# Feed-forward products as 2x2 blocks with seven products on two token chunks, middle features through DRAM

## The chip, the core and the metric

The kernel runs on one core of a Trainium2 chip. The metric is the time of one execution on the device, in microseconds (us), taken as the median of three runs. Five engines work side by side, each through its own instruction queue in order: TensorE (PE, matrix products, with its weight loads PEld), VectorE (DVE), ScalarE (ACT), GpSimd (POOL) and SyncE (SP, which here issues most transfers). Work of different engines is ordered by semaphores. Operands lie in SBUF (128 partitions), products accumulate in PSUM (8 banks), and everything else lies in DRAM.

## What is computed

One inference step of a two-layer decoder trunk: 1024 prompt tokens and 32 sample tokens, together T = 1056 columns, with 1024 features. Each layer mixes tokens (a recurrence, windowed attention, two gated branches), normalizes, and then runs the feed-forward part, which is all that changes here:

```python
x = layer_norm(ALPHA * x + mix @ P['w_out'], P['ln1_g'], P['ln1_b'])
h = jnp.square(jax.nn.relu(x @ P['w_ff_up']))
x = layer_norm(ALPHA * x + h @ P['w_ff_down'], P['ln2_g'], P['ln2_b'])
```

`w_ff_up` is 1024 x 4096 and `w_ff_down` is 4096 x 1024. All is float32.

## The kernel before

**Layout.** Activations are feature-major: a tile holds 128 features by the tokens of one chunk. The chunks `CH` are 384, 384 and 288 tokens wide. x is 8 such tiles per chunk (`KD`), the 4096 middle features are 32 (index f), in 8 groups of G = 4.

**Precision.** A float32 factor is split into a high part in a reduced format (`fp32r`) and the rest: `split` for activations and `wsplit` for weights do a cast on ACT (L257, L223) and a subtraction on DVE (L258, L224). A product is three matmuls: high x high, high x low, low x high. So one tile of 128 x 128 weights against one chunk costs three matmuls with 384 or 288 columns. `gemm_parts` (L233) issues them into one PSUM bank, and takes the banks of `gbanks` in turn: in the feed-forward part `mm` and `c`, two banks each.

**Feed-forward, `ff` (L1311).** For each group of 4 middle rows, `up` makes h for each row and chunk (24 matmuls; ACT takes the relu out of PSUM at L1320, DVE squares at L1321, then `split`), and h stays in SBUF. Then `down` adds that group's part to each of the 8 output rows (12 matmuls; DVE adds the bank to the accumulator in SBUF at L1335). One raw weight tile of 128 x 1024 is loaded by SP (L214) per up row and per pair of output rows, two raw buffers deep, and split into one of four weight tiles (three in `wp`, one in the small pool).

**Order.** Tile's scheduler orders the instructions of every engine at build time by readiness and by their order in the program. Inside `manual_schedule` PE's order is that of the program: there the rest of the output projection (`tail`), the three parts of the first normalization (booked into the stream of matmuls by `book` at the times `LN_TIMES`) and the first three up rows are woven. At the end the last group's `down` is woven with the second normalization in the same way. In between no POOL instruction is used.

**Slots.** `Slots` hands out SBUF tiles by chunk: `outer` 16 and `inner` 20 for each of the three chunks. `layer_norm` takes the sums on DVE and POOL and, for the first normalization, writes x as high and low parts (L337 to L342) and gives the float32 tile back (`acc[k].put()`).

Of the kernel before, what the change touches and what calls it, by code (L numbers as in the profile page):

```python
# [10 lines left out]
F32 = mybir.dt.float32  # L11
# [6 lines left out]
L = 2  # L18
# [92 lines left out]
class Kern:  # L111
    def __init__(self, tc, i, o, ctx):
# [15 lines left out]
        self.wpools = deque([self.wp])  # L128
        self.gbanks = deque([(self.mm, "mm")])
# [27 lines left out]
        self.d_g = [dt(f"d_g{l}", (16, 128, T)) for l in range(L)]  # L157

# [52 lines left out]

    def wraw(self, src):
        raw = self.rp.tile([128, 1024], F32, tag="raw", name=self.nm("raw"))
        self.nc.sync.dma_start(out=raw, in_=src)  # L214
        return raw

    def wsplit(self, raw):
        nc = self.nc
        pool = self.wpools[0]
        self.wpools.rotate(-1)  # L220
        w = pool.tile([128, 2, 8, 128], F32R, tag="w", name=self.nm("w"))
# [14 lines left out]
    def gemm_parts(self, w, k0, rhs, n):  # L236

        p = self.ps(*self.gbanks[0])
        self.gbanks.rotate(-1)
        nk = len(rhs)  # L240
        for k in range(nk):
            hi, lo = rhs[k]
            wh, wl = w[:, 0, k0 + k, :], w[:, 1, k0 + k, :]
            for j, (a, b) in enumerate(((wh, hi), (wh, lo), (wl, hi))):
                self.mmul(p[:, :n], lhsT=a, rhs=b[:, :n], start=(k == 0 and j == 0),
                          stop=(k == nk - 1 and j == 2))
                yield
        return p

# [35 lines left out]
    def layer_norm(self, tmp, small, acc, s, c, gcol, bcol, out=None, last=False):  # L285
# [47 lines left out]
        for k in range(KD):  # L333
# [3 lines left out]
            if out is None:  # L337
                hi, lo = self.outer.get(c, F32R), (self.outer if self.outer.free[c] else tmp).get(c, F32R)
# [3 lines left out]
                acc[k].put()  # L342
# [890 lines left out]
    def mix(self, l, inner, small):  # L1233
# [67 lines left out]
        def tail(c):  # L1301
# [4 lines left out]
            self.book(self.layer_norm(inner, small, [xf[k][c] for k in range(KD)], sums[c], c, P_L1G, P_L1B), LN_TIMES)  # L1306

        return tail


    def ff(self, l, inner, small, tail):  # L1311
        nc, tc, i = self.nc, self.tc, self.i
        ng = 32 // G
        sums = [None] * 3

        def up(w, h, f, c):
            n = CH[c][1]
            p = yield from self.gemm_parts(w, 0, self.xr(c), n)
            z, hi, lo = inner.get(c), inner.get(c, F32R), inner.get(c, F32R)
            nc.scalar.activation(out=z.f, in_=p[:, :n], func=AF.Relu)  # L1320
            nc.vector.tensor_tensor(z.f, z.f, z.f, op=ALU.mult)  # L1321
            self.split(z.f, hi.t, lo.t)
            z.put()
            h[f, c] = (hi, lo)

        def down(w, h, m, c, gi):
# [3 lines left out]
            if gi == 0:  # L1330
                hi, lo = self.x[m][c]
                nc.vector.scalar_tensor_tensor(a, hi.f, ALPHA, p[:, :n], op0=ALU.mult, op1=ALU.add)
                nc.vector.scalar_tensor_tensor(a, lo.f, ALPHA, a, op0=ALU.mult, op1=ALU.add)
            else:
                nc.vector.tensor_tensor(a, a, p[:, :n], op=ALU.add)  # L1335

        for gi in range(ng - 1):
            h = {}
            if gi == 0:
                with tc.manual_schedule(engines={mybir.EngineType.PE}):  # L1340
                    for c in range(3):
                        self.weave(tail(c))
                    ws = [self.wload(i["w_up"][l, f]) for f in range(3)]
                    for c in range(3):
                        for f in range(3):
                            self.weave(up(ws[f], h, f, c))
                    self.due()
                acc = [[inner.get(c) for c in range(3)] for _ in range(KD)]
            for f in range(3 if gi == 0 else 0, G):
                w = self.wload(i["w_up"][l, gi * G + f])  # L1350
                for c in range(3):
                    drain(up(w, h, f, c))
            for mp in range(4):
                w = self.wload(i["w_down"][l, gi, mp])
                for m in (2 * mp, 2 * mp + 1):
                    for c in range(3):
                        drain(down(w, h, m, c, gi))
            for f, c in h:
                for t in h[f, c]:
                    t.put()  # L1360
        h = {}
        self.wpools = deque([self.wp] * 3 + [small])
        for f in range(G):
            w = self.wload(i["w_up"][l, gi * G + G + f])
            for c in range(3):
                drain(up(w, h, f, c))
        ws = [self.wload(i["w_down"][l, ng - 1, mp]) for mp in range(4)]
        for r in self.x:
            for a, b in r:
                a.put()  # L1370
                b.put()
        self.x = [[None] * 3 for _ in range(KD)]
# [5 lines left out]
        with tc.manual_schedule(engines={mybir.EngineType.PE}):  # L1378
            for c in range(3):
                for m in range(KD):  # L1380
                    self.weave(down(ws[m // 2], h, m, c, ng - 1))
                    self.add_up(inner, sums, acc, m, c)
# [11 lines left out]
    def run(self):  # L1394
        nc, tc, i = self.nc, self.tc, self.i
        self.x = [[None] * 3 for _ in range(KD)]
        for l in range(L):
# [6 lines left out]
            with ExitStack() as ctx:  # L1404
# [4 lines left out]
                self.wpools = deque([self.wp] * 3 + [sp])  # L1409
                self.gbanks = deque([(self.mm, "mm"), (self.pc, "c")])  # L1410
                self.ff(l, inner, sp, self.mix(l, inner, sp))
            self.wpools = deque([self.wp])
            self.gbanks = deque([(self.mm, "mm")])
# [149 lines left out]
```

## Time and profile before

| | us |
|---|---|
| median of three runs | 3591.2 (3590.25 to 3594.06) |
| the profiled execution, its own time | 3581.97 |
| its span, first to last instruction | 3579.8 |
| PE busy | 3476.0 (97%) |
| DVE, ACT, POOL busy | 1980.9, 1100.0, 655.7 |

The profile is one execution. "Busy" of PE counts matmuls that overlap; how fast PE really goes is read from the chain of work, where 24 matmuls in a row have one length. The granted clock (PEclk) is a share of full speed. The feed-forward parts are the stretches from about 1020 to 1790 us and from about 2790 us to the end.

### The profile page before, as it was taken

How to read it: one execution, taken by the hardware profiler on the slowest of the kernel's cores; microseconds unless marked ns; L12 is line 12 of the kernel's file. 1: busy time of each engine (PE TensorE's matmuls, PEld its weight loads, DVE VectorE, ACT ScalarE, POOL GpSimd, SP SyncE). 2: the span in 40 equal slices, each digit the busy share in tenths (PEclk: the TensorE clock that was granted, in tenths of full speed). 3: DMA queues.
4: the chain of work that ended last, by engine and by line, in shares of the span. 5: the costliest groups of instructions: out<-in, count | busy, mean ns of one | idle time of the engine just before them, and what ended most of it. 6: DMA issues, size and time to landing. Idle time of an engine off the chain costs nothing.

```text
span 3579.8 us, 63696 instructions
## 1 busy us (share of the span) xinstructions
PE 3476.0 (97%) x25286; PEld 3226.5 (90%) x25286; DVE 1980.9 (55%) x5216; ACT 1100.0 (31%) x2553; POOL 655.7 (18%) x1014
## 2 busy tenths in 40 slices
PE   8999999998989999999999999999999899999997
PEld 8688888888989999999987888888799899999997
DVE  4746777756465333333657478777573643333335
ACT  4654332222152122212347443322221422221222
POOL 2223423210140000000342334232102300000002
PEclk9999999999999999999999999999899999999998
DMA  5124233325111111111131333222351111111111
GB/s 169 61 91 116 77 83 81 85 72 183 59 30 48 48 48 44 46 48 48 34 86 49 102 103 92 78 79 83 109 154 36 42 48 48 47 43 48 48 42 49
DMA packets 213225, 255.45 MB, mean 71 GB/s; under 512 B 103488, under 2 KB 175712, under 8 KB 212896
## 3 DMA queue, kind: packets, MB, share of 16 engines
q1 hardware_dynamic: 184032, 211.31, 20.3%
q10 hardware_dynamic: 27360, 35.57, 2.7%
q8 instruction: 199, 3.26, 0.4%
q0 software_dynamic: 1536, 4.52, 0.3%
q14 instruction: 98, 0.80, 0.1%
HBM read 188.99 MB, written 58.95 MB: 69 GB/s over the span
## 4 chain that ended last, share of the span: by engine, by line
PE 84%; DVE 5%; issue 1%; POOL 1%; ACT 1%; DMA 1%; SPq 0%; ACTq 0%; DVEq 0%; POOLq 0%
PE mm L202 44%; PE c L202 30%; PE b L202 8%; PE b L206 1%; DMA i<-d_ya 0%; PE c L206 0%; PE b L759 0%; DVE pd L985 0%; DVE Xt L987 0%; DVE x L1260 0%; POOL x L341 0%; DMA i<-d_yr 0%; DVE ln L270 0%; DVE ln L271 0%; DVE A L1022 0%
## 5 line engine op out<-in xcount | busy, mean ns | idle before, releaser
L202 PE MATMUL mm<-x,w 128*128 128x384 f32 (+1 forms) x7680 | 1439.4, 333 | 15.6 <-ACT x L257 6.8
L202 PEld LDWEIGHTS mm<-x,w 128*128 128x128 f32 x7680 | 1238.9, 190 | 68.9 <-issue 12.5
L202 PE MATMUL mm<-i,w 128*128 128x384 f32 (+1 forms) x3264 | 584.9, 323 | 17.4 <-ACT i L257 17.4
L202 PE MATMUL c<-i,w 128*128 128x384 f32 (+1 forms) x3264 | 582.4, 323 | 0.8 <-DVE i L1275 0.6
L202 PEld LDWEIGHTS mm<-i,w 128*128 128x128 f32 x3264 | 533.8, 189 | 21.1 <-ACT i L257 17.6
L202 PEld LDWEIGHTS c<-i,w 128*128 128x128 f32 x3264 | 534.2, 188 | 3.5 <-DVE i L1275 1.2
L223 ACT CAST w<-raw 128x1024 fp32r<-128x1024 f32 x232 | 243.0, 1048 | 738.3 <-PE c L202 526.2
L202 PE MATMUL c<-x,w 128*128 128x384 f32 (+1 forms) x2496 | 439.1, 324 | 0.0
L202 PEld LDWEIGHTS c<-x,w 128*128 128x128 f32 x2496 | 410.3, 190 | 0.4 <-DVE x L258 0.4
L224 DVE TENSOR_TENSOR w<-raw,w 128x1024 fp32r<-128x1024 f32 x232 | 287.1, 1237 | 98.0 <-ACT w L223 96.3
L1321 DVE TENSOR_TENSOR i<-i 128x384 f32<-128x384 f32 (+1 forms) x192 | 101.1, 527 | 348.0 <-ACT i L1320 348.0
L283 POOL TENSOR_TENSOR i<-i,i 128x384 f32<-128x384 f32 (+1 forms) x36 | 36.4, 1012 | 1377.1 <-DVE i L1335 1372.9
L1335 DVE TENSOR_TENSOR i<-i,c 128x384 f32<-128x384 f32 (+1 forms) x168 | 87.3, 520 | 197.2 <-PE c L202 197.2
L1335 DVE TENSOR_TENSOR i<-i,mm 128x384 f32<-128x384 f32 (+1 forms) x168 | 87.0, 518 | 133.8 <-PE mm L202 133.7
L258 DVE TENSOR_TENSOR i<-i,i 128x384 fp32r<-128x384 f32 (+1 forms) x216 | 116.9, 545 | 77.6 <-ACT i L257 77.5
L257 ACT CAST i<-i 128x384 fp32r<-128x384 f32 (+1 forms) x216 | 104.7, 486 | 91.2 <-DVE i L1321 80.9
L787 POOL TENSOR_TENSOR z<-z,gs 128x384 f32<-128x384 f32 (+1 forms) x84 | 80.1, 953 | 287.2 <-issue 185.2
L1320 ACT ACTIVATE i<-mm 128x384 f32<-128x384 f32 (+1 forms) x96 | 44.7, 465 | 208.5 <-PE mm L202 208.5
L1103 DVE SCALAR_TENSOR_TENSOR S<-c,eL,sd 64x64 f32<-64x64 f32 x256 | 72.4, 283 | 63.3 <-PE c L202 58.9
L1320 ACT ACTIVATE i<-c 128x384 f32<-128x384 f32 (+1 forms) x96 | 44.7, 465 | 200.6 <-PE c L202 200.6
L1093 DVE COPY sav<-c 64x128 f32<-64x128 f32 x128 | 36.8, 288 | 125.3 <-PE c L202 124.3
L1079 POOL TENSOR_SCALAR sd<-S,eL 128x128 f32<-128x128 f32 x128 | 96.8, 757 | 49.2 <-DVE S L1103 46.2
(278 smaller groups left out, 3982.8 us busy)
## 6 DMA issues: line engine op xcount, KB each, us to landing
raw<-in_w_in_dram SPq DMA_DIRECT2D x72, 512.0 KB
raw<-in_w_up_dram SPq DMA_DIRECT2D x64, 512.0 KB
raw<-in_w_down_dram SPq DMA_DIRECT2D x64, 512.0 KB
d_g<-gs ACTq DMA_DIRECT2D x64, 192.0 KB
i<-d_g SPq DMA_DIRECT2D x64, 192.0 KB
d_z<-z ACTq DMA_DIRECT2D x52, 192.0 KB
raw<-in_w_out_dram SPq DMA_DIRECT2D x16, 512.0 KB
qrot<-qraw SPq DMA_DIRECT2D x40, 132.0 KB
```

Of the source, the lines that this page charges most:

```text
L202: return self.nc.tensor.matmul(out, lhsT=lhsT, rhs=rhs, start=start, stop=stop)
L223: nc.scalar.copy(wf[:, 0, :], raw)
L224: self.weng.tensor_tensor(wf[:, 1, :], raw, wf[:, 0, :].bitcast(F32), op=ALU.subtract)
L257: self.nc.scalar.copy(hi, src)
L258: self.nc.vector.tensor_tensor(lo, src, hi.bitcast(F32), op=ALU.subtract)
L787: nc.gpsimd.tensor_tensor(out[:, :n], out[:, :n], prev[:, :n], op=ALU.add)
L1079: nc.gpsimd.tensor_scalar(sd, S0, ecol, None, op0=ALU.mult)
L1093: nc.vector.tensor_copy(sav[B, :], sa[B, 0:128])
L1103: nc.vector.scalar_tensor_tensor(S1[r, r], pS[r, 0:64], ecol[r, :], sd[r, r], op0=ALU.mult, op1=ALU.add)
L1320: nc.scalar.activation(out=z.f, in_=p[:, :n], func=AF.Relu)
L1321: nc.vector.tensor_tensor(z.f, z.f, z.f, op=ALU.mult)
L1335: nc.vector.tensor_tensor(a, a, p[:, :n], op=ALU.add)
```

## The change

The feed-forward products over the first two chunks (384 tokens each) are made as 2 x 2 blocks with seven block products in place of eight. For **up**, a pair of middle rows (f, f+1) is one side of the block, the two halves of x's 8 tiles the other, and the two chunks the third. For **down**, a pair of output rows, two and two of a group's 4 middle tiles, and the two chunks. Chunk 2 (288 tokens) keeps its plain products, and so do the first 4 up rows and the last down group.

What comes with it:

- `tokens_up` makes four differences of x per k (8 on POOL, 8 on DVE) and splits them, once in a layer; x must stay in float32 until then (`keep`, which also stores it in DRAM as `d_x`, from where `residual` loads it).
- `weights_up` makes for each pair of rows four sums of 128 x 512 on POOL, and splits 3.5 weight tiles in place of 2. `weights_down` makes four sums of 128 x 256 on POOL for each pair of output rows and splits 2 tiles in place of 1.
- The banks are combined on their way out: `pair_up` has an ACT copy, 7 DVE additions and 2 ACT relus per pair, then relu (ACT) and square (POOL) for the four tiles in `store`; every middle tile goes to DRAM (`d_h`).
- `tokens_down` loads a group's 12 middle tiles back, makes 8 differences of 128 x 384 on POOL, and splits 14 tiles of 384 and 4 of 288 columns. It comes after the group before in the program.
- `pair_down` keeps seven accumulators per pair of output rows (`E`), with one DVE addition per block product; chunk 2 goes out by an ACT copy and a POOL addition (in group 0 by one DVE instruction). `finish` combines the seven after group 6.
- Four more buffers: raw tiles and weight tiles also in the small pool (4 and 5 in all), and seven-product banks in the order `mm`, `b`, `c`, `b`, so all 8. The DMA scratch is cut to 2048 bytes.

```diff
 def wraw(self, src):
-        raw = self.rp.tile([128, 1024], F32, tag="raw", name=self.nm("raw"))
+        raw = self.rtile()
...
+    def products(self, ops, n):
+        p = self.ps(*self.gbanks[0])
+        self.gbanks.rotate(-1)
+        e = len(ops) - 1
+        for q, (w, k, (hi, lo)) in enumerate(ops):
+            for j, (a, b) in enumerate(((0, hi), (0, lo), (1, hi))):
+                self.mmul(p[:, :n], lhsT=w[:, a, k, :], rhs=b.t[:, :n], start=(q == 0 and j == 0), stop=(q == e and j == 2))
+        return p[:, :n]
...
-                acc[k].put()
+                if keep is None:
+                    acc[k].put()
+                else:
+                    nc.sync.dma_start(out=keep[k, :, c0:c0 + n], in_=a[k])
...
+        def store(z, f, c):
+            nc.scalar.activation(out=z.f, in_=z.f, func=AF.Relu)
+            P(z.f, z.f, z.f, op=ALU.mult)
+            nc.sync.dma_start(out=d_h[f, :, cols(c)], in_=z.f)
+            z.put()
...
+        def tokens_up():
+            x0, x1 = [xf[k][0] for k in range(KD)], [xf[k][1] for k in range(KD)]
+            for k in range(4):
+                P(x0[k].f, x1[k].f, x0[k].f, op=ALU.subtract)
+                V(x1[k].f, x1[4 + k].f, x1[k].f, op=ALU.subtract)
+                P(x1[4 + k].f, x1[4 + k].f, x0[k].f, op=ALU.subtract)
+                V(x0[4 + k].f, x1[4 + k].f, x0[4 + k].f, op=ALU.subtract)
+                for t, z in ((1, x0[k]), (3, x1[k]), (2, x1[4 + k]), (4, x0[4 + k])):
+                    B[t].append(self.parts(z, lambda: get(0)))
+        def sums_w(a, b, s):
+            P(s[0], b[0], b[1], op=ALU.add)
+            P(s[1], s[0], a[0], op=ALU.subtract)
+            P(s[2], a[0], b[0], op=ALU.subtract)
+            P(s[3], a[1], s[1], op=ALU.subtract)
...
+        def weights_up(f):
+            raw, raw2, s1, s2 = self.wraw(i["w_up"][l, f]), self.wraw(i["w_up"][l, f + 1]), self.rtile(), self.rtile()
+            q = lambda t: [t[:, 0:512], t[:, 512:1024]]
+            sums_w(q(raw), q(raw2), q(s1) + q(s2))
+            a = self.wsplit(raw)
+            d = small.tile([128, 2, 4, 128], F32R, tag="wd", name=self.nm("wd"), bufs=2)
+            self.split(raw2[:, 512:1024], half(d, 0), half(d, 1))
+            return a, self.wsplit(s1), self.wsplit(s2), d
+        def pair_up(W, f, last):
...
+            ACTC(u.f, self.products(ops(a, 0, B[11]), n))
+            V(z.f, u.f, self.products(ops(a, 4, B[21]), n), op=ALU.add)
+            store(z, f, 0)
+            p = self.products(ops(a, 0, x2[:4]) + ops(a, 4, x2[4:]), CH[2][1])
...
+            V(u.f, u.f, self.products(ops(s12, 4, B[2]), n), op=ALU.add)
+            V(v.f, u.f, self.products(ops(s34, 0, B[3]), n), op=ALU.add)
+            p = self.products(ops(s12, 0, B[1]), n)
+            V(u.f, u.f, p, op=ALU.add)
+            V(z.f, v.f, p, op=ALU.add)
+            store(z, f + 1, 1)
+            V(u.f, u.f, self.products(ops(s34, 4, B[22]), n), op=ALU.add)
+            store(u, f, 1)
+            V(v.f, v.f, self.products(ops(d, 0, B[4]), n), op=ALU.subtract)
+            store(v, f + 1, 0)
+            p = self.products(ops(s12, 0, x2[:4]) + ops(d, 0, xd), CH[2][1])
...
+        def tokens_down(g):
+            r = [[load(G * g + k, c) for k in range(G)] for c in range(3)]
+            t1, t2, t3, t4 = [[get(0) for _ in range(2)] for _ in range(4)]
+            for k in range(2):
+                P(t1[k].f, r[1][k].f, r[0][k].f, op=ALU.subtract)
+                P(t3[k].f, r[1][2 + k].f, r[1][k].f, op=ALU.subtract)
+                r[1][k].put()
+                P(t2[k].f, r[1][2 + k].f, t1[k].f, op=ALU.subtract)
+                P(t4[k].f, t2[k].f, r[0][2 + k].f, op=ALU.subtract)
+            for t, c, z in ((11, 0, r[0][:2]), (21, 0, r[0][2:]), (0, 2, r[2]), (2, 0, t2), (3, 0, t3), (1, 0, t1),
+                            (22, 0, r[1][2:]), (4, 0, t4)):
+                H[t] = [self.parts(z[k], lambda: get(c)) for k in range(len(z))]
...
+        def pair_down(W, H, g, mp, last):
+            for t, w, k0, b in ((1, a, 0, 11), (2, a, 2, 21), (0, a, 0, 0), (6, s, 2, 2), (7, s, 4, 3), (5, s, 0, 1),
+                                (3, s, 6, 22), (4, a, 6, 4), (8, a, 4, 0)):
+                if t in (0, 8):
...
+                        ACTC(z.f, p)
+                        P(acc[m][2].f, acc[m][2].f, z.f, op=ALU.add)
...
+                else:
+                    p = self.products(ops(w, k0, H[b]), n)
...
+                        V(e, e, p, op=ALU.add)
...
+        self.gbanks = deque([(self.mm, "mm"), (self.pb, "b"), (self.pc, "c"), (self.pb, "b")])
+        W = weights_up(G)
+        for f in range(G, 32, 2):
+            Wn = weights_up(f + 2) if f < 30 else None
+            pair_up(W, f, f == 30)
+            W = Wn
...
+        W = weights_down(0, 0)
+        H = tokens_down(0)
+        for g in range(ng - 1):
             for mp in range(4):
...
+                if (g, mp) != (ng - 2, 3):
+                    Wn = weights_down(g + (mp == 3), (mp + 1) % 4)
+                pair_down(W, H, g, mp, mp == 3)
+                W = Wn
+                if g == ng - 2:
+                    finish(mp)
+            if g < ng - 2:
+                H = tokens_down(g + 1)
         h = {}
...
+        for c in range(3):
+            for f in range(G):
+                h[f, c] = self.parts(load(32 - G + f, c), lambda: inner.get(c, F32R))
```

## Rows read from the trace of the kernel before

**Rows 1.** The page: busy time of the engines; the chain by engine.
```profile
PE 3476.0 (97%) x25286; PEld 3226.5 (90%) x25286; DVE 1980.9 (55%) x5216; ACT 1100.0 (31%) x2553; POOL 655.7 (18%) x1014
...
PE 84%; DVE 5%; issue 1%; POOL 1%; ACT 1%; DMA 1%; SPq 0%; ACTq 0%; DVEq 0%; POOLq 0%
```

**Rows 2.** Busy time by stretch: length, PE, PEld, DVE, ACT, POOL, PEclk, DMA share, GB/s.
```profile
1000.00:1100.00 100.00, 87.61 (x531) 86.27 (x530) 66.88 (x134) 45.94 (x96) 31.79 (x32) 0.93 0.14 43
1200.00:1300.00 100.00, 100.00 (x628) 100.00 (x627) 36.38 (x61) 18.96 (x32) 0.00 (x0) 1.00 0.15 48
```

**Rows 3.** The chain in order of time: start, length, engine, bank, line, matmuls.
```profile
1224.55 4.16 PE c L202 x24
1228.71 3.19 PE mm L202 x24
```

**Rows 4.** Groups by form, DVE and ACT: busy us, mean ns; idle before.
```profile
L224 DVE TENSOR_TENSOR w<-raw,w 128x1024 fp32r<-128x1024 f32 x232 | 287.1, 1237 | 98.0 <-ACT w L223 96.3 <-issue 0.3
L223 ACT CAST w<-raw 128x1024 fp32r<-128x1024 f32 x232 | 243.0, 1048 | 738.3 <-PE c L202 526.2 <-issue 138.5 <-PE mm L202 59.6
...
L258 DVE TENSOR_TENSOR i<-i,i 128x384 fp32r<-128x384 f32 x144 | 83.9, 588 | 76.2 <-ACT i L257 76.2
L257 ACT CAST i<-i 128x384 fp32r<-128x384 f32 x144 | 73.6, 513 | 87.5 <-DVE i L1321 80.9 <-DMA i<-d_ya 6.3
...
L1335 DVE TENSOR_TENSOR i<-i,c 128x384 f32<-128x384 f32 x112 | 62.0, 553 | 147.2 <-PE c L202 147.2
...
L258 DVE TENSOR_TENSOR i<-i,i 128x288 fp32r<-128x288 f32 x72 | 33.0, 459 | 1.4 <-ACT i L257 1.3
...
L1320 ACT ACTIVATE i<-c 128x288 f32<-128x288 f32 x32 | 13.2, 412 | 49.8 <-PE c L202 49.8
```

**Rows 5.** Groups by form, POOL: additions and products of two SBUF operands.
```profile
L453 POOL TENSOR_TENSOR qh<-qraw,qh 64x1024 fp32r<-64x1024 f32 x16 | 41.0, 2562 | 21.7 <-ACT qh L452 21.1
...
L283 POOL TENSOR_TENSOR i<-i,i 128x384 f32<-128x384 f32 x24 | 24.3, 1013 | 1374.8 <-DVE i L1335 1372.5 <-DVE ln L271 2.0
L787 POOL TENSOR_TENSOR z<-z,gs 128x288 f32<-128x288 f32 x28 | 22.8, 814 | 77.9 <-issue 72.6 <-ACT shout L786 5.3
```

**Rows 6.** The page: mean GB/s of the transfers, in 40 slices of the span.
```profile
GB/s 169 61 91 116 77 83 81 85 72 183 59 30 48 48 48 44 46 48 48 34 86 49 102 103 92 78 79 83 109 154 36 42 48 48 47 43 48 48 42 49
```

**Rows 7.** Timeline 1034 to 1045 us: start, length, engine, line, tiles (DVE and POOL).
```profile
1034.69 7.33 POOL L341 TENSOR_TENSOR x<-x,x 128x384 fp32r<-128x384 f32 x6
...
1036.23 1.93 DVE L224 TENSOR_TENSOR w<-raw,w 128x1024 fp32r<-128x1024 f32 x1
...
1040.04 0.92 DVE L271 SCALAR_TENSOR_TENSOR ln<-ln,ln_v 128x3 f32<-128x3 f32 x1
...
1042.07 0.16 DVE L271 SCALAR_TENSOR_TENSOR ln<-ln,ln_v 128x3 f32<-128x3 f32 x1
```

**Rows 8.** Timeline 1763 to 1770 us, POOL and DVE.
```profile
1763.15 3.96 POOL L341 TENSOR_TENSOR x<-i,x 128x384 fp32r<-128x384 f32 x4 [1.75 <-ACT x L340]
...
1765.09 0.54 DVE L1335 TENSOR_TENSOR i<-i,mm 128x384 f32<-128x384 f32 x1
1765.55 0.55 DVE L1335 TENSOR_TENSOR i<-i,c 128x384 f32<-128x384 f32 x1
...
1768.09 1.33 DVE L283 TENSOR_TENSOR i<-i,i 128x384 f32<-128x384 f32 x1 [1.53 <-POOL i L283]
```

**Rows 9.** Timeline 1044 to 1053 us, PE alone: a wait and the matmuls after it.
```profile
1044.58 1.46 PE L202 MATMUL b<-ident,ln_rb 128*128 128x128 f32 x6 [4.71 <-DVE ln_rb L327]
1045.86 6.44 PE L202 MATMUL c<-x,w 128*128 128x384 f32 x22
...
1052.48 3.97 PE L202 MATMUL mm<-x,w 128*128 128x384 f32 x22
```

**Rows 10.** Busy time by stretch around that wait (columns as in rows 2).
```profile
1040.00:1050.00 10.00, 5.42 (x19) 5.45 (x20) 8.98 (x22) 6.10 (x15) 4.94 (x6) 0.71 0.11 43
```

More of the change, by code (lines that the diff above doesn't have):

```diff
@@ new lines, in release, with load @@
+        def release(pairs):
+            for p in pairs:
+                for t in p:
+                    t.put()
+        def load(f, c):
+            z = get(c, F32)
+            nc.sync.dma_start(out=z.f, in_=d_h[f, :, cols(c)])
+            return z
+        def tokens_down(g):
+            r = [[load(G * g + k, c) for k in range(G)] for c in range(3)]
+            H = {}
+            t1, t2, t3, t4 = [[get(0) for _ in range(2)] for _ in range(4)]
[8 more added lines that the diff above has]
+                H[t] = [self.parts(z[k], lambda: get(c)) for k in range(len(z))]
+            return H
@@ new lines, in finish @@
+        def finish(mp):
+            e = {t: E[mp, t] for t in range(1, 8)}
+            V(e[2].f, e[2].f, e[1].f, op=ALU.add)
+            V(e[6].f, e[6].f, e[1].f, op=ALU.add)
+            V(e[7].f, e[7].f, e[6].f, op=ALU.add)
+            V(e[4].f, e[7].f, e[4].f, op=ALU.subtract)
+            P(e[6].f, e[6].f, e[5].f, op=ALU.add)
+            P(e[3].f, e[3].f, e[6].f, op=ALU.add)
+            P(e[5].f, e[5].f, e[7].f, op=ALU.add)
+            e[1].put()
+            e[6].put()
+            e[7].put()
+            x = residual(2 * mp + 1, 1, self.outer)
+            nc.vector.scalar_tensor_tensor(e[5].f, x.f, ALPHA, e[5].f, op0=ALU.mult, op1=ALU.add)
+            x.put()
+            acc[2 * mp][0], acc[2 * mp][1], acc[2 * mp + 1][0], acc[2 * mp + 1][1] = e[2], e[3], e[4], e[5]
@@ L1327, in down @@
+        def down(w, h, m, c):
             n = CH[c][1]
@@ L1329, in down @@
             a = acc[m][c].f
[L1330 to L1352, printed above, removed]
-            for mp in range(4):
[L1354 to L1360, printed above, removed]
@@ L1361, in ff @@
-        h = {}
[L1362 to L1366, printed above, removed]
-        ws = [self.wload(i["w_down"][l, ng - 1, mp]) for mp in range(4)]
[L1368 to L1372, printed above, removed]
+            nc.vector.tensor_tensor(a, a, p[:, :n], op=ALU.add)
@@ new lines, in ff @@
+        B = {t: [] for t in (1, 2, 3, 4)}
+        with tc.manual_schedule(engines={mybir.EngineType.PE}):
+            for c in range(3):
+                self.weave(tail(c))
+            ws = [self.wload(i["w_up"][l, f]) for f in range(G)]
+            for c in range(3):
+                for f in range(G):
+                    self.weave(up(ws[f], f, c))
+                if c == 0:
+                    tokens_up()
+            self.due()
+        x = self.x
+        release([x[k][1] for k in range(4)])
@@ L1374, in norm @@
+        h = {}
+        for c in range(3):
+            for f in range(G):
+                h[f, c] = self.parts(load(32 - G + f, c), lambda: inner.get(c, F32R))
+        self.wpools = deque([small] * 2 + [self.wp] * 2)
+        ws = [self.wload(i["w_down"][l, ng - 1, mp]) for mp in range(4)]
+        self.gbanks = deque([(self.mm, "mm"), (self.pc, "c")])
+        sums = [None] * 3
         def norm(c, last=False):
```

131 lines of the change are left out of this document (113 added, 18 removed).

## The prediction

> **What bounds the kernel now.** Four views, in this order. The page's first part says that PE is busy for 97% of the span and every other engine for at most 55%, and the chain of work gives PE 84% [rows 1]. The stretches of 100 us say where: inside the feed-forward loop PE is busy for all of each stretch, at the full granted clock, with DVE at 36%, ACT at 19% and no POOL instruction at all [rows 2]. Around the first normalization it is not: 12.4 us of 100 are idle there. The chain gives PE's real pace: 24 matmuls of 384 columns take 4.16 us, 24 of 288 columns 3.19 us [rows 3], so 173.3 and 132.9 ns each. Last, the groups say who waits for whom: the weight casts on ACT and the additions out of PSUM on DVE stand idle for PE [rows 4], not the reverse. So in the feed-forward loop a matmul less is its full time less, as long as the other engines stay behind PE.
>
> **What is removed.** In each layer up has 14 pairs of rows and two chunks of 384: before 2 x 2 x 24 = 96 matmuls, after 7 x 12 = 84. Down has 28 pairs of output rows in groups 0 to 6: before 48, after 42. That is 14 x 12 + 28 x 6 = 336 a layer, 672 in all, at 173.3 ns: **-116.5 us**. Chunk 2 keeps its count.
>
> **Up: what is added, for one pair.** PE needs 84 x 0.1733 + 48 x 0.1329 = 20.9 us (23.0 before). DVE: 3.5 weight subtractions at 1.237 and 7 additions at 0.553 [rows 4]: 8.2 us. ACT: 3.5 casts at 1.048, a copy and six relus at about 0.5: 7.1 us. POOL: no row has 512 columns; 1024 took 2.562 us, 384 took 1.013 [rows 5], so between them 512 is 1.32 us. Four sums and four squares at 1.013 and two at 0.814: 11.0 us. Each is far below 20.9, and banks leave room: eight in turn are over 16 us of PE work, and the weights are prepared one pair ahead. So I cost all of this at nothing, hidden under PE; if that cover went, the first thing late would be the third weight sum. Stores and loads are 86 MB over both layers' 1600 us, some 54 GB/s beside about 48, where 183 were moved in other slices [rows 6]. SP issues six stores and two loads a pair; a store that waits for its POOL square holds back the next raw load behind it, which has most of a pair to spare.
>
> **Down: for one group** (four pairs of output rows) PE needs 4 x (42 x 0.1733 + 24 x 0.1329) = 41.9 us (46.0 before). DVE: 28 additions at 0.553, 8 weight subtractions at 1.237, 14 token splits at 0.588 and 4 at 0.459: 15.5 + 9.9 + 10.1 = 35.5 us [rows 4]. POOL: 16 sums of 256 columns (from 0.814 at 288 on the same line, 0.74), 8 additions of 0.814, 8 token differences of 1.013: 11.8 + 6.5 + 8.1 = 26.4 us. ACT: 8 casts at 1.048, 14 at 0.513, 4 and 8 copies near 0.41: 20.5 us. Taken singly all are below PE.
>
> **But DVE and POOL are not single.** In the normalization, where both work at once, the same DVE instruction on 3 columns takes 0.16 us, and 0.92 us beside a running POOL instruction; a weight subtraction takes 1.93 in place of 1.237; and six POOL instructions take 7.33 us [rows 7] where four took 3.96 us, so 1.4 us more than 5.94: about that one subtraction. An addition out of SBUF alone took 1.33 us behind POOL [rows 8]. But additions with one input in PSUM kept their 0.54 us beside the same POOL work [rows 8]. So these rows say: a DVE instruction with both inputs in SBUF and a POOL instruction exclude one another for their whole length. Additions out of PSUM are free of it. The Trainium skill ("SBUF — State Buffer", "Who interferes with whom") states this: the second of the two blocks until the first is done. The trace agrees, with 0.92 against 0.16 us. Without that rule the engines' own sums would decide, and down would cost nothing; with it, two columns add up.
>
> They add up so. Up: 11.0 + 4.3 = 15.3 of 20.9 us, still hidden. Down: 26.4 on POOL and 9.9 + 10.1 = 20.0 on DVE are **46.4 us against PE's 41.9**. With DVE's starts as close as 0.46 us where 0.55 is the duration [rows 8], 26 instructions give back 2.3: 44.1. So down becomes bound by the pair of DVE and POOL, by 2.2 to 4.5 us a group.
>
> Where does that show? At the border between groups. The 28 slots for the next group's split tokens are those of the group that PE still reads, since 28 of them, 28 accumulators and 16 loads and differences are just the 72 there are. In the order in which slots come back, four of the eight differences wait for the last pair's first product, so the POOL chain of 8.1 us starts about 9 us before PE is through, beside that pair's weight sums (3.0) and chunk 2's additions (1.6), and the splits (10.1 on DVE) follow it. DVE has in the two pairs around the border 10.1 + 4.9 + 7.7 = 22.7 of 20.9 us, without its waits for POOL. Queued behind a split that waits are PE's evictions; the eight banks cover some 8 us of that. A wait of 4.5 us at each of 6 borders in 2 layers is **+54 us**. Bounds: nothing, if loads and differences run so early that all of it hides; 11 us a border (below) if they run late.
>
> **Three transitions.** First: the part woven with the first normalization has four up rows in place of three; `tokens_up` (8 POOL, 8 DVE differences, 16 splits, about 22 us on the shared pair) lies beside some 46 us of PE work, but the normalization's small DVE steps, which already make PE wait 4.71 us [rows 9], may be held back by it, while 12 splits of h leave. I take 0, between -4 and +5 a layer. Second: up to down, the first group's splits lie under the last pair of up, where no weights are prepared: 1 us a layer, 0 to 4. Third: the last group's 12 splits (6.5 us on DVE) and four weight tiles were hidden under up rows; now only under the last pair's 10.5 us, beside `finish`: 4 us a layer, 0 to 10. Together **+10 us**.
>
> **Sum:** -116.5 + 54 + 10 = -52.5 us. The profiled execution has 3582.0 us (span 3579.8 and 2.2 around it), so 3529.5; the median of the runs shown is 1.0026 times that execution: **3539 us**.
>
> **Rivals.** (A) *Everything hides.* For it: singly no engine passes 36 of 41.9 us, and the middle pairs of each group leave the two engines slack for work done early. Against it: 44.1 to 46.4 us of shared work. Price: -116.5 + 2: 3467.5, or 3476 us. (B) *Slower: the border runs in series.* If the differences stand behind the last pair's chunk 2 addition on POOL, which waits for PE's last product, then after it come a copy (0.41), the addition (0.81), 8.1 us of differences and the first split of a difference (0.51 + 0.59): 10.4 us, of which PE has 1.04 + 1.04 + 1.6 = 3.7 us of products whose tokens need no difference. PE stands 6.7 us. After a stand of 4.71 us the granted clock was 0.71 in that stretch [rows 10], and 22 matmuls took 6.44 in place of 3.97 us [rows 9]: 2.5 more. With 1.8 us for the other ten splits, which POOL's next weight sums hold up, that is 11 us, 132 in all: -116.5 + 132 + 10 = +25.5, so 3617 us. It decides from (116.5 - 10)/12 = 8.9 us a border. For it: POOL and DVE run in order, and the program has the differences behind that addition. Against it: the scheduler orders by readiness, and the slots of the loads and of four differences are free a group ahead. (C) *The gain doesn't come in up either*: if the chain raw load, four sums (5.3), cast (1.05), subtraction (1.24) is late by 2 us in each of 28 pairs, another 56 us are gone: +3.5, so 3595 us. Against it: 15.3 of 20.9 us on the shared pair, and a pair's time ahead.
>
> **How the numbers follow.** Forecast 0.58, with its own range of 3505 to 3580 (2 to 8 us a border); A 0.13; B 0.17; C 0.12. The range reaches over A's time and into the lower half of B: 3476 to 3605. A measurement of this kernel can tell about 0.2%, 7 us, from no change. Faster by more: forecast, A and two fifths of C, 0.76. Same: the rest of C, 0.07. Slower: B, 0.17.
>
> **What would show it.** In the profile after: 28 pairs of up at 20.9 us with PE full (right) or gaps before PE released by a DVE or ACT weight tile (C). In down, groups near 46 us with one wait of some us each at the border, released by a split out of `parts`, and DVE subtractions of tokens and weights at clearly more than 0.588 and 1.237 us (right); at 41.9 us (A); at 50 and more with POOL's differences after the last product and a granted clock below 1 there (B). The matmul count must fall by 672 from 25286. The prediction is wrong if the shared pair of DVE and POOL is not what PE waits for in down, or if the slower stretches are those of the normalizations.

## The result and the profile after

The changed kernel took 3613.6 us (median of four runs, 3610.25 to 3616.31), the kernel before 3592.4 beside it: a ratio of 1.0059 with a 95% interval of 1.0042 to 1.0076. It is 21 us slower, where 3539 was forecast, and the time lies above the range. Rival B named this side and 3617 us; only half of its reason holds (see below).

The page of the profile after, its first part and the chain by engine (for the rows of before see [rows 1]):

```profile
PE 3404.5 (94%) x24614; PEld 3147.4 (87%) x24614; DVE 2304.1 (64%) x5528; ACT 1308.7 (36%) x2945; POOL 1458.8 (40%) x1774
...
PE 73%; DVE 10%; POOL 4%; issue 2%; ACT 2%; DMA 1%; SPq 0%; ACTq 0%; DVEq 0%; POOLq 0%
```

PE has 672 matmuls less, as foreseen, and holds 73% of the chain where it held 84%. The stretches of time tell where it went: up, then down, then the first normalization (columns as in rows 2):

```profile
1150.00:1350.00 200.00, 200.00 (x1261) 200.00 (x1260) 81.86 (x108) 66.54 (x107) 107.16 (x97) 1.00 0.32 101
...
1550.00:1600.00 50.00, 43.38 (x260) 43.15 (x259) 36.09 (x54) 17.51 (x34) 29.24 (x31) 0.93 0.27 86
...
1000.00:1100.00 100.00, 75.29 (x443) 73.66 (x443) 80.17 (x136) 49.52 (x106) 63.61 (x54) 0.86 0.27 91
```

Up is PE's alone: full for 200 us at full clock, with POOL and DVE working beside it. Down is not: 43.4 of 50 us, at a granted clock of 0.93. Nor is the normalization: 75.3 of 100 us where it was 87.6 [rows 2]. The list of PE's waits over the whole span (total, times, longest, in us) names the tiles. The first line is of the kernel before, where the waits for a split on DVE (L258) came to 1.2 us in all; the others are of the kernel after:

```profile
PE b L202 <- DVE ln_rb L327: 20.4, 9, 4.7
...
PE mm L205 <- DVE x L287: 60.1, 12, 6.7
PE b L205 <- DVE ln_rb L356: 43.7, 9, 12.6
...
PE mm L205 <- DVE w L236: 6.5, 2, 4.4
```

**Down.** The starts of one and the same chunk 2 product in successive groups, read from PE's timeline, are 42.0, 51.3, 51.0, 50.9, 51.1 and 50.7 us apart in layer 1 (43.2, 50.5, 50.3, 51.2, 51.1 and 50.9 in layer 2); PE's own work is 41.9. One such border, PE first, then DVE, ACT and POOL (start, length, engine, line, tiles; in brackets the idle time before it and what ended it):

```profile
1483.11 0.43 PE L205 MATMUL mm<-x,w 128*128 128x288 f32 x2
1488.25 0.85 PE L205 MATMUL mm<-x,w 128*128 128x288 f32 x2 [4.72 <-DVE x L287]
1488.90 0.52 PE L205 MATMUL b<-x,w 128*128 128x384 f32 x1
1489.22 0.52 PE L205 MATMUL b<-i,w 128*128 128x384 f32 x1
...
1479.92 0.56 DVE L287 TENSOR_TENSOR x<-i,x 128x384 fp32r<-128x384 f32 x1 [4.47 <-ACT x L286]
...
1486.49 1.71 DVE L287 TENSOR_TENSOR x<-x,x 128x384 fp32r<-128x384 f32 x2
...
1478.25 0.51 ACT L286 CAST i<-i 128x384 fp32r<-128x384 f32 x1 [5.51 <-POOL i L1468]
...
1484.14 0.39 ACT L1501 COPY x<-b 128x288 f32<-128x288 f32 x1
...
1484.61 1.07 POOL L1502 TENSOR_TENSOR i<-i,x 128x288 f32<-128x288 f32 x1 [4.68 <-DMA i<-d_h]
```

PE stands in the middle of the third product of the new group, the plain one of chunk 2 (288 columns). It waits for the low part of the fourth of the group's four chunk 2 tiles. The split that makes it is the second of the two in the row at 1486.49, 1.24 us long. In DVE's order it comes after 14 of the group's 18 splits, seven of which PE needs later.

What keeps it there is the tile that it writes. `Slots` hands out tiles in the order in which they were given back in the program, and so the two parts of the fourth token go into the tiles that held the copies (L1501) of the last two chunk 2 products of the group before. Such a tile is free only when the addition on POOL (L1502) has read it. PE was through with the last of these products at about 1477.8; its copy stands on ACT at 1484.14, the addition on POOL ends at 1485.68, and in the program the split waits for this addition. (The addition itself waits in the program for the copy alone; the DMA in its brackets is how the view accounts for the idle time.) The copy was late because it stands in ACT's queue behind the cast at 1478.25, which had waited 5.51 us for a difference on POOL (L1468), and then a dozen more instructions. The same late cast held up DVE for 4.47 us at 1479.92. The token's load had been issued 30 us before.

After the wait the matmuls start 0.32 us apart in place of 0.173 [rows 3], for some 4 us: after PE had stood 4.72 us the granted clock from 1488.3 to 1492.3 us is 0.50, the lower of its two levels (1.2 in place of 2.4 GHz).

**The first normalization.** From its first `ln_rb` tile to its third 42.3 us passed before and 56.9 pass now, in both layers. In the kernel before, PE's wait for the second tile, and the first and last of DVE's instructions that make the third:

```profile
1027.70 0.91 PE L202 MATMUL b<-ident,ln_rb 128*128 128x128 f32 x6 [1.36 <-DVE ln_rb L327]
...
1036.15 0.16 DVE L324 TENSOR_SCALAR ln_v<-b 128x3 f32<-128x3 f32 x1
...
1043.88 0.55 DVE L327 COPY ln_rb<-ln 128x384 f32<-128x384 f32 x1
```

In the kernel after, PE's waits for the second and the third tile, then DVE and POOL before the third:

```profile
1033.84 1.62 PE L205 MATMUL b<-ident,ln_rb 128*128 128x128 f32 x6 [5.18 <-DVE ln_rb L356]
...
1060.85 1.46 PE L205 MATMUL b<-ident,ln_rb 128*128 128x128 f32 x6 [12.62 <-DVE ln_rb L356]
...
1044.52 0.16 DVE L353 TENSOR_SCALAR ln_v<-b 128x3 f32<-128x3 f32 x1 [3.64 <-PE b L205]
...
1053.72 0.95 DVE L300 SCALAR_TENSOR_TENSOR ln<-ln,ln_v 128x3 f32<-128x3 f32 x1
1054.68 1.34 DVE L1385 TENSOR_TENSOR x<-x,x 128x384 f32<-128x384 f32 x1
1055.95 1.34 DVE L1374 TENSOR_TENSOR i<-i 128x384 f32<-128x384 f32 x1
1057.21 0.95 DVE L301 SCALAR_TENSOR_TENSOR ln<-ln,ln 128x3 f32<-128x3 f32 x1
...
1058.55 0.15 DVE L299 TENSOR_TENSOR ln<-ln 128x3 f32<-128x3 f32 x1
...
1060.17 0.54 DVE L356 COPY ln_rb<-ln 128x384 f32<-128x384 f32 x1
...
1055.57 2.57 POOL L1384 TENSOR_TENSOR x<-x,x 128x384 f32<-128x384 f32 x2
```

The two waits were 1.36 and 4.71 us before [rows 9]; they are 5.18 and 12.62. The second grows by as much as the chain of small DVE steps before it: 7.7 us from its first to its last row above before, 15.7 now. A small step takes 0.95 us while POOL works, on the lower parts of the normalized x (L370) or on the differences of `tokens_up` (L1384), and 0.15 as soon as POOL is through. But of the nine steps of the iteration four took 0.84 to 0.99 us in the kernel before too, and six take 0.94 to 0.97 now: that is 1.7 us. The other 6.2 us are DVE's own work. One instruction stood between the steps before; now there are twelve, and nine of them are the differences (L1383, L1385) and splits of `tokens_up`.

### The profile page after: what moved, and what is told of

Read it like the earlier page. It is cut to its first block, busy times and chain, and to the rows that moved or that the text cites. A ratio compares the mean times of both kernels' runs of the same rounds, so it can differ in the third digit from the quotient of the medians.

```text
span 3611.0 us, 65605 instructions
## 1 busy us (share of the span) xinstructions
PE 3404.5 (94%) x24614; PEld 3147.4 (87%) x24614; DVE 2304.1 (64%) x5528; ACT 1308.7 (36%) x2945; POOL 1458.8 (40%) x1774
## 4 chain that ended last, share of the span: by engine, by line
PE 73%; DVE 10%; POOL 4%; issue 2%; ACT 2%; DMA 1%; SPq 0%; ACTq 0%; DVEq 0%; POOLq 0%
PE mm L205 32%; PE b L205 21%; PE c L205 19%; DVE i L287 1%; PE b L209 1%; DVE w L236 1%; DVE x L287 1%; DVE i L1517 1%; DMA d_g<-gs 0%; PE c L209 0%; PE b L791 0%; DVE pd L1017 0%; POOL i L1502 0%; DVE x L1292 0%; DVE ln L300 0%
## 5 line engine op out<-in xcount | busy, mean ns | idle before, releaser
L205 PEld LDWEIGHTS mm<-x,w 128*128 128x128 f32 x6536 | 1062.7, 191 | 131.1 <-DVE x L287 63.5
L205 PE MATMUL mm<-i,w 128*128 128x384 f32 (+1 forms) x2044 | 419.4, 331 | 29.6 <-ACT i L286 16.1
L205 PE MATMUL c<-i,w 128*128 128x384 f32 (+1 forms) x2090 | 425.9, 330 | 3.2 <-DVE i L1498 1.8
L205 PE MATMUL b<-x,w 128*128 128x384 f32 (+1 forms) x1770 | 398.5, 319 | 0.9 <-ACT x L1514 0.9
L205 PE MATMUL b<-i,w 128*128 128x384 f32 (+1 forms) x1590 | 387.1, 332 | 1.7 <-DVE i L1498 1.7
L205 PEld LDWEIGHTS mm<-i,w 128*128 128x128 f32 x2044 | 350.2, 192 | 32.6 <-ACT i L286 16.3
L205 PEld LDWEIGHTS c<-i,w 128*128 128x128 f32 x2090 | 358.0, 192 | 6.5 <-DVE i L1498 2.5
L205 PEld LDWEIGHTS b<-x,w 128*128 128x128 f32 x1770 | 298.3, 192 | 1.5 <-ACT x L1514 1.5
L205 PEld LDWEIGHTS b<-i,w 128*128 128x128 f32 x1590 | 284.8, 192 | 2.3 <-DVE i L1498 2.3
L205 PEld LDWEIGHTS c<-x,w 128*128 128x128 f32 x1330 | 227.3, 195 | 4.7 <-ACT x L286 3.6
L1502 POOL TENSOR_TENSOR i<-i,x 128x288 f32<-128x288 f32 x96 | 103.5, 1078 | 145.4 <-ACT x L1501 140.7
```

Of the source, the lines that this page charges most:

```text
L205: return self.nc.tensor.matmul(out, lhsT=lhsT, rhs=rhs, start=start, stop=stop)
L1502: P(acc[m][2].f, acc[m][2].f, z.f, op=ALU.add)
```

## The experiments

Theory: two separate losses, the *place* of chunk 2's fourth token at the borders of down, and the work of `tokens_up` on POOL and DVE among the small steps of the first normalization. Rival: DVE and POOL together are simply full in down, so order changes nothing.

**Chunk 2 early.** Loads and splits of the next group's chunk 2 move ahead of the last pair of the group before, so that they no longer get the tiles of that pair's copies:

```diff
+        def chunk_2(g):
+            return [self.parts(z, lambda: get(2)) for z in [load(G * g + k, 2) for k in range(G)]]
...
+                if mp == 3 and g < ng - 2:
+                    H0 = chunk_2(g + 1)
                 pair_down(W, H, g, mp, mp == 3)
...
-                H = tokens_down(g + 1)
+                H = tokens_down(g + 1, H0)
```

> Loads and splits of the next group's chunk 2 stand ahead of the last pair of the group before; all else as in the changed kernel. In that kernel PE stands 5.9 us on average at ten borders for the low part of one tile, the fourth token of chunk 2, and then runs some 3 us at half clock; a group takes 51.0 us. Theory (place: that token is loaded and split last although PE needs it third): this wait goes, a smaller one for a split of a difference or none takes its place, 0 to 3 us; a group takes 43 to 47 us, the time falls to 3520 to 3570. Rival (the shared pair of DVE and POOL is full: 46.4 us of work besides evictions): the wait only moves to another split, a group stays at 49 to 51 us, the time at 3595 to 3615.

3562.7 us, ratio to the kernel before 0.9933 (0.9906 to 0.9961). The long waits at the token are gone; what is left at a border is 1 to 3 us, for an addition out of a bank. Two stretches of 50 us:

```profile
1550.00:1600.00 50.00, 47.53 (x295) 46.13 (x294) 43.64 (x63) 18.41 (x35) 31.74 (x33) 1.00 0.31 96
1600.00:1650.00 50.00, 48.82 (x303) 47.91 (x303) 41.34 (x64) 20.63 (x38) 38.20 (x39) 1.00 0.28 85
```

From its timeline, PE and DVE:

```profile
1581.57 0.40 PE L205 MATMUL c<-x,w 128*128 128x288 f32 x1 [0.93 <-DVE x L1520]
...
1581.90 1.73 DVE L236 TENSOR_TENSOR w<-raw,w 128x1024 fp32r<-128x1024 f32 x1
```

The clock is full and a group takes 43.9 to 45.6 us in the middle of the part (49 at the last border). The work on DVE and POOL is the same, only the place differs: it is the larger cause. What is left looks like the shared pair: a subtraction of 1024 columns beside POOL takes 1.73 us, 1.24 alone [rows 4].

**All early.** The loads and the eight differences move ahead of the last pair too; the 14 splits of 384 columns stay behind it (against the run with chunk 2 early):

```diff
                 if mp == 3 and g < ng - 2:
-                    H0 = chunk_2(g + 1)
+                    R = loads_down(g + 1)
...
+            return r, t1, t2, t3, t4, chunk_2(g)
```

> As the run with chunk 2 early, and the loads and the eight differences of the other two chunks stand ahead of the last pair as well, in the 16 tiles that are free then; only the 14 splits stay behind it. Theory (place): a group takes 42 to 46 us, 3510 to 3560, and if a wait is left it is shorter than with chunk 2 alone. Rival (shared pair full): 49 to 51 us a group, 3595 to 3615, however the work is ordered. If differences behind the last product were what matters, as rival B of the prediction has it, this run gains 3 us a border or more on the one before.

3601.9 us, 1.0042 (1.0027 to 1.0057): the time of the rival, for another reason. DVE and POOL at a border, then PE:

```profile
1542.64 1.33 DVE L287 TENSOR_TENSOR i<-x,x 128x288 fp32r<-128x288 f32 x1 [4.03 <-ACT x L286]
1549.46 1.03 DVE L287 TENSOR_TENSOR x<-i,x 128x288 fp32r<-128x288 f32 x1 [5.48 <-POOL i L1509]
...
1543.61 2.21 POOL L1470 TENSOR_TENSOR i<-i,i 128x384 f32<-128x384 f32 x2
...
1548.63 1.54 POOL L1509 TENSOR_TENSOR i<-i,x 128x288 f32<-128x288 f32 x2
...
1551.00 1.39 PE L205 MATMUL c<-i,w 128*128 128x384 f32 x4 [4.80 <-DVE x L1524]
```

DVE is not full: it stands 4.03 and 5.48 us at two splits of chunk 2. The second is kept by POOL's addition (L1509 here), which now comes behind the differences and the weight sums on POOL. The evictions stand behind that split, so PE waits for a bank. Work done earlier on POOL delayed the one POOL step that gives the tile back.

**Weight sums of down taken off POOL.** The four sums of a pair are left out, and ACT copies the raw tile in their place:

```diff
-            sums_w([q(raw, 0), q(raw, 1)], [q(raw, 2), q(raw, 3)], [q(s, k) for k in range(4)])
+            ACTC(s, raw)
```

> In down the four weight sums of a pair are left out: ACT copies the raw tile into the tile of the sums instead, so POOL does 11.8 us a group less, and down is not computed rightly. DVE's order stays that of the changed kernel, with the fourth token of chunk 2 behind 14 splits. Rival (shared pair of DVE and POOL): 46.4 - 11.8 = 34.6 us, PE's 41.9 bound a group, the border waits go, 3490 to 3530. Theory (place): the wait at that token stays, at most 2 us shorter; a group takes 48 to 51 us, 3580 to 3615.

3589.0 us, 0.9992 (0.9976 to 1.0009), as the theory has it. PE still stands at the same tile, 4.46 us in place of up to 6.7, and groups take 48.1 to 49.5 us:

```profile
1582.35 0.85 PE L205 MATMUL mm<-x,w 128*128 128x288 f32 x2 [4.46 <-DVE x L287]
```

By groups of 51.0 us in the changed kernel, 48.8 here and 44.5 with chunk 2 early (the last border left out), POOL's load is worth 2.2 us of a border and the place 6.5.

**Both.** Chunk 2 early and the sums off POOL.

> Chunk 2 early, and the weight sums of down left out (ACT copies the raw tile in their place, so down is not computed rightly): POOL does 11.8 us a group less with the fourth token in its better place. With chunk 2 early a group took 43.7 to 45.4 us in its middle, against 41.9 of PE work. If what is left there is the shared pair of DVE and POOL (46.4 us of work, 34.6 without the sums), a group falls to 41.9 to 42.6 us and the time by 20 to 30 us below that of chunk 2 early, to 3533 to 3543. Rival (DVE's own queue at the border): 43.5 us a group or more, 3555 or more.

3541.0 us, 0.9850 (0.9824 to 0.9876), within the time expected, while groups of 42.5 to 43.9 us lie above the 42.6 that the shared pair alone would give. With the place mended the sums on POOL cost about 1.4 us a group; the last 1.3 over PE's 41.9 are not explained by them. These groups lie on both sides of the 43.5 us that the rival, DVE's own queue, had named, so it is not shown which of the two holds what is left.

**Chunk 2's sum straight out of PSUM**, nothing moved:

```diff
-                        z = get(2)
-                        ACTC(z.f, p)
-                        P(acc[m][2].f, acc[m][2].f, z.f, op=ALU.add)
-                        z.put()
+                        V(acc[m][2].f, acc[m][2].f, p, op=ALU.add)
```

> Chunk 2's product is added by one DVE instruction straight out of PSUM, without the copy on ACT and the addition on POOL; nothing is moved in the program. POOL does 6.5 us a group less, DVE 3.7 more, and the loads of the next chunk 2 no longer take tiles that wait for POOL, so their splits come ahead of the last pair by themselves. Theory (place): the wait at the fourth token goes as with chunk 2 early, a group takes 43 to 46 us, 3545 to 3570. Rival (DVE's own queue sets the border, since it holds splits, evictions and subtractions in order): 3.7 us more on DVE make it worse than that run, 47 to 51 us a group, 3575 to 3615.

3539.4 us, 0.9855 (0.9833 to 0.9878): better than either expectation. No tile of chunk 2 waits for POOL, its four splits move ahead of the last pair by themselves, and POOL has less to do. Groups take 42.1 to 43.5 us: PE's pace.

**The differences of x late.** A column of zero that comes from the third chunk is added to x, so that `tokens_up` can't start before that chunk is normalized:

```diff
+            nc.vector.tensor_scalar(zero, xf[0][2].f[:, 0:1], 0.0, None, op0=ALU.mult)
+            for k in range(4):
+                V(x0[k].f[:, 0:1], x0[k].f[:, 0:1], zero, op=ALU.add)
...
-                if c == 0:
-                    tokens_up()
             self.due()
+        tokens_up()
```

> The differences of x are held back until the third chunk is normalized, by one column added as zero that comes from that chunk; nothing else is changed. In the changed kernel PE waits 17.8 and 17.3 us for the two ln_rb tiles of a first normalization, 6.1 in the kernel before, and does 15 us less work in the 100 us around it. Theory (these differences, on POOL and DVE, hold up the normalization's small steps): ln_rb waits fall back to 6 to 9 us a layer, the time by 18 to 30 us, to 3583 to 3596. Rival (the work on DVE and POOL in that stretch is too much wherever it stands): the waits come back in the first pairs of up, the time stays within 8 us of 3613.

3599.3 us, 1.0024 (1.0011 to 1.0037), 14 us less than the changed kernel, below the 18 to 30 expected. PE's two waits, and two of DVE's small steps:

```profile
1036.30 1.62 PE L205 MATMUL b<-ident,ln_rb 128*128 128x128 f32 x6 [5.19 <-DVE ln_rb L356]
1053.00 0.91 PE L205 MATMUL b<-ident,ln_rb 128*128 128x128 f32 x6 [2.83 <-DVE ln_rb L356]
...
1050.17 0.92 DVE L301 SCALAR_TENSOR_TENSOR ln<-ln,ln 128x3 f32<-128x3 f32 x1
...
1051.51 0.16 DVE L301 SCALAR_TENSOR_TENSOR ln<-ln,ln 128x3 f32<-128x3 f32 x1
```

The second wait falls from 12.62 to 2.83 us; from the first `ln_rb` to the third 46.6 us pass in place of 56.9. The first wait stays, so the differences are not its cause; and up to the second normalization 2.3 and 3.5 us are given back.

**Combinations.** Chunk 2 early and the differences late:

> Chunk 2 early, and the differences of x late. If the two causes are separate their gains add up: 3613.6 - 51 - 14 = 3549, within 3543 to 3556. If the later differences of x only push DVE's work into the first pairs and from there on, less than 8 us of the 14 come on top: 3556 or more.

3540.4 us, 0.9859 (0.9838 to 0.9880): the gains add up, and 9 us more than their sum are left unexplained. Then the three edits together:

> Chunk 2 early, its sum straight out of PSUM, and the differences of x late. Theory (with the place mended the rest of a border, 43.6 to 45 us against 41.9, is DVE's queue held up by POOL: a subtraction of 1024 columns took 1.73 and 1.80 in place of 1.24 there): 6.5 us less of POOL work for 3.7 us of additions that POOL does not touch give back 0 to 2 us a group: 3525 to 3549. Rival (DVE is full at the border, 10 of 10 us, by its own work): 3.7 us more cost 1 to 3 us a group, 3556 to 3585.

3508.2 us, 0.9771 (0.9750 to 0.9793), and 0.9794 (0.9778 to 0.9810) once more on another chip: about 2% faster than the kernel before. Both times, 3508.2 and 3518.7 us, lie below the range of the theory, by 17 and 6 us. Down is PE's alone:

```profile
1550.00:1600.00 50.00, 49.95 (x316) 49.63 (x315) 43.11 (x72) 19.23 (x36) 34.77 (x32) 1.00 0.33 99
```

Without the move of chunk 2:

> Chunk 2's sum straight out of PSUM and the differences of x late, without moving chunk 2 in the program. Theory (once no tile of chunk 2 waits for POOL, its place mends itself, so moving it adds nothing): groups of 42.1 to 43.5 us and 3508 to 3520, the time of the three edits within 10 us. Rival (the early place is worth something of its own): 3521 or more.

3513.7 us, 0.9773 (0.9755 to 0.9791), the same. Once no tile of chunk 2 waits for POOL, no gain of the move can be told.

**Blocks in up alone**, down plain out of DRAM, without and with the differences late:

```diff
+                h[f, c] = self.parts(load(G * g + f, c), lambda: get(c))
...
+            p = self.gemm(w, (m % 2) * 4, [(h[f, c][0].t, h[f, c][1].t) for f in range(G)], n)
...
+                V(acc[m][c].f, acc[m][c].f, p[:, :n], op=ALU.add)
```

> Blocks only in up; down makes its 96 plain products a group and adds each straight out of PSUM, but takes h from DRAM and splits 12 tiles a group. Theory (up keeps its 58.2 us, the first normalization loses 28 to 30 over both layers, all else that was lost lies at the borders of down): 3592 - 58 + 29 = 3563, and up to 10 us for the loads and the last group's splits: 3560 to 3575. Rival C of the prediction (the gain of up is lost as well): 3590 or more.

> Blocks only in up, and the differences of x late: prices the blocks of down with their border mended against the plain down. Groups of plain down took 46.0 us, blocks 42.3 with the three edits, 12 of them 44 us; the end of a layer, with seven accumulators to be combined, took 50.5 us after the last block group and 40.4 after the last plain one, which takes back 20. If so, 3557.6 - 14 to 20 = 3538 to 3544, some 24 to 36 us above the three edits. Rival (blocks of down bring nothing net even when mended): 3500 to 3515.

3557.6 us, 0.9903 (0.9868 to 0.9938), and 3535.2 us, 0.9842 (0.9816 to 0.9867), each 2 to 3 us below its range. Up keeps its gain; rival C falls. A stretch of down in the first of them:

```profile
1550.00:1600.00 50.00, 50.00 (x314) 50.00 (x313) 23.56 (x42) 9.73 (x16) 0.00 (x0) 1.00 0.29 89
```

Plain groups take 46.0 us with PE full. The blocks of down, mended, bring 3535.2 - 3513.7 = 21 us net on one chip, where 58 us of matmuls go.

**The end of the layer.** In the changed kernel 43.4 and 40.9 us pass from the start of the last chunk 2 product of the seventh group to the second normalization's first `ln_rb`, with up alone 34.6. The row of the longest wait names a weight tile:

```profile
1743.60 3.57 PE L205 MATMUL mm<-i,w 128*128 128x384 f32 x10 [4.42 <-DVE w L236]
```

The three edits with these weight tiles ahead of the last group's splits:

```diff
+        ws = [self.wload(i["w_down"][l, ng - 1, mp]) for mp in range(4)]
         h = {}
...
-        ws = [self.wload(i["w_down"][l, ng - 1, mp]) for mp in range(4)]
```

> The three edits, and in the program the four weight tiles of the last group stand ahead of its 12 token splits. In the three edits PE waits 1.89 us for the subtraction of such a tile and 1.98 us for one of DVE's additions before it. Theory (the end of the layer is late by these waits on DVE): 2 to 4 us a layer less, 3500 to 3505. Rival (DVE is full there, so another of its instructions is late instead): within 3505 to 3512, no difference that can be told.

3517.2 us, 0.9781 (0.9753 to 0.9809): no difference that can be told. In the first layer the wait for DVE's addition is 0.93 us where it was 1.98, the one for the weight tile 4.00 where it was 1.89. But the three edits' own second layer has 1.32 and 4.20, so this is no more than they vary by themselves. DVE has work nearly all the time there, with 0.55 us idle from 1686 to 1700 us in the three edits; that its queue is what makes the end late is not shown.

**The first pair's weight sums late**, in the same way as the differences, beside the three edits alone:

```diff
+            if f == G:
+                for r in (raw, raw2):
+                    V(r[:, 0:1], r[:, 0:1], Z[0], op=ALU.add)
+                    V(r[:, 512:513], r[:, 512:513], Z[0], op=ALU.add)
```

> The three edits once more, beside the next run on the same chip: 3505 to 3520, ratio to the kernel before 0.975 to 0.980.

> The three edits, and the four weight sums of the first pair of up are held back in the same way until the third chunk is normalized. In the changed kernel the second normalization's ln_rb kept PE waiting 5.18 us (1.36 before), the differences of x held back left 5.19, and POOL ran these sums just then, with small DVE steps of 1.21 us. Theory (the sums on POOL hold up the small steps): that wait falls to 1 to 2 us, the time by 6 to 10 us against the three edits. Rival (the first pair of up needs its weights by then): the wait comes back ahead of the first pair, and the time stays within 4 us of the three edits.

3518.7 and 3519.1 us, ratios 0.9794 (0.9778 to 0.9810) and 0.9800 (0.9785 to 0.9816). PE's waits with the sums late:

```profile
1042.71 0.91 PE L205 MATMUL b<-ident,ln_rb 128*128 128x128 f32 x6 [1.36 <-DVE ln_rb L356]
1057.85 0.83 PE L205 MATMUL b<-ident,ln_rb 128*128 128x128 f32 x6 [2.95 <-DVE ln_rb L356]
1091.10 3.39 PE L205 MATMUL mm<-x,w 128*128 128x288 f32 x13 [5.16 <-ACT i L1373]
```

The wait that was left falls from 5.18 to 1.36 us: these sums were its cause. But a wait of 2.13 us at 1084.63, for a bank in the last up rows, is now 5.16. The theory holds for the wait, the rival for the time.

## Why the prediction was wrong, point by point

- **What is removed, -116.5 us: right.** 672 matmuls less, up full at full clock, up alone 35 us faster, where its 336 are worth 58 less the first normalization's 29.
- **Down's border, +54 us: mis-sized, and the step that failed is the place.** A wait of 4.5 us at each border was worked out from the shared pair's sum alone. Measured: five of six borders in each layer cost about 9 us, and one of them nearly nothing: 45.6 and 45.8 us a layer over 6 x 41.9, 91 in all. I summed the work of DVE and POOL and set it against PE. I followed the slots of the 384-column tiles and the differences, but not those of chunk 2's four tokens, though PE needs them third. Nor did I see that their tiles come back only after a copy on ACT and an addition on POOL. With the place mended a group took 43.9 to 45.6 us, near the shared pair's 44.1 to 46.4. That fits the sum, but does not show it to be the cause: with 11.8 us of it taken away a group still took 42.5 to 43.9. The Trainium skill ("SBUF — State Buffer", "Who interferes with whom") states the exclusion that the sum rests on, and the runs agree (0.95 against 0.15 us above). For the place the Trainium skill has another sentence ("Perfetto Trace Analysis", "Tensor Engine Instruction (MATMUL, LD_WEIGHTS)"): ACT, DVE and GPSIMD take their instructions strictly in order. The trace with all moved early agrees: DVE stood 5.48 us at one split with PE's evictions behind it.
- **The clock at a border: left out of the forecast.** I counted it in rival B alone (2.5 us). A stand of 4.7 us was followed by matmuls 0.32 us apart at a granted clock of 0.50, some 1.7 us more at that border; in the middle of down the granted clock was 0.93 on average, and 1.00 once the waits were gone.
- **First normalization, 0 a layer: wrong, +14.6 and +14.7.** I had the mechanism and its rows (0.92 in place of 0.16 us), and still set it at nothing between -4 and +5. What I costed as work beside PE stood inside the chain of small steps: the second wait grew by 7.9 us, 1.7 of them for two more steps held up by POOL, 6.2 for DVE's own instructions between the steps. The first wait grew by 3.8, by the weight sums of the first pair of up, which the scheduler had put among the steps and which I had costed as hidden.
- **Up to down 1, last group 4 a layer: right in size.** PE waits 1.7 and 2.9 us at the first; the last group costs 8.8 and 6.3 us over plain down, within the 0 to 10 given.
- **The sum.** -116.5 + 91.4 + 29.3 + 15.1 + 4.6 = +24. The profiled spans differ by 31 (3579.8 and 3611.0); 8 us of that lie in stretches without an edit (+8.2 in the next layer's attention, +1.7 before the first normalization, -2.0 in the second). The attention alone takes between 960 and 976 us in the executions profiled here.
- **Rival B.** Its side was right, and so is the start of its chain: the copy and the POOL addition of the last pair's chunk 2 product. But what stands behind that addition is the split of the fourth chunk 2 token, not the differences: with chunk 2 alone moved, and the differences left where they were, the wait went. Its 132 us at the borders were 91, below its threshold of 106.5 (8.9 a border). Without the first normalization's 29 us the sum is -5, about no change; those made the kernel slower. That its 3617 us lies so near the measured time is luck.

## What to carry to other kernels

Set engine sums against each other only after following, tile by tile, what the consumer needs first: where its producer stands in each in-order queue, and which engine gives back the buffer that its load goes into. A buffer whose release hangs on the most loaded engine passes that engine's lateness on to loads, then to splits, then to every eviction queued behind them; adding out of PSUM directly took out the copy, the addition and the wait at once. And a chain of small instructions on the path is not to be shared with a bulk stream: price it by the longer duration of the steps that are held up, and by every instruction that its own engine may run between them. Here the second was the larger.

## What the runs showed of the hardware

What a stand of PE costs behind it, beyond its own length. After 4.72 us of waiting (at the border shown above) the matmuls started 0.32 us apart before the pace of 0.173 came back, 1.7 us more, at a granted clock of 0.50. Four more stands, two in the three edits, one in the run with the weights first, and one in the run with the sums off POOL:

```profile
1689.37 3.81 PE L205 MATMUL mm<-i,w 128*128 128x384 f32 x12 [1.98 <-DVE x L1521]
...
1697.81 2.03 PE L205 MATMUL mm<-i,w 128*128 128x384 f32 x10 [1.89 <-DVE w L236]
...
1696.01 3.57 PE L205 MATMUL mm<-i,w 128*128 128x384 f32 x10 [4.00 <-DVE w L236]
...
3498.35 2.03 PE L205 MATMUL mm<-i,w 128*128 128x384 f32 x10 [3.30 <-DVE w L236]
```

After 4.00 us ten matmuls took 3.57 us, at a granted clock of 0.50; after 1.89 and after 3.30 us they took 2.03 at 1.00. So the stands of 4.0 and 4.7 us cost some 35 to 40% more than their own length, and those of 1.89 and 3.30 us little beyond it. But the length does not decide it alone: after 1.98 us twelve matmuls took 3.81 us, at a granted clock of 0.61 over the next 4 us. What does is not shown here.
